# Decoder layer, last third: down projection product by product over all columns, first gate and up pair as plain products, all sums on VectorE

## Chip, core and metric

One core of a Trainium2 chip. The metric is the device time of one execution in microseconds (us), the median of several runs. Engines by the names of the profile: PE (TensorE matrix multiply), PEld (its weight loads), DVE (VectorE), ACT (ScalarE), POOL (GpSimd), SP (SyncE, whose queue issues all the DMAs).

## What is computed

One layer of a decoder trunk on x of 1024 tokens by 1024 channels in float32: a norm, one input projection, three attention mixers, a gated merge and an output projection with a residual, then a feed-forward block with a residual. The change lies in the last third, from the merge of the last mixer on:

```python
proj = jnp.einsum('btnm,nmd->btnd', branches, w_branch[l])
gates = jax.nn.sigmoid(cols['merge']).reshape(b, t, N_BRANCH, D_MODEL)
x = x + (gates * proj).sum(axis=2) @ w_out[l]
h = rms_norm(x, norm_ffn[l])
a = h @ w_gate[l]                                  # 1024 x 2816
a = causal_depthwise_conv(a, conv_w[l]) + conv_b[l]  # width 3 along the tokens
x = x + (gelu(a) * (h @ w_up[l])) @ w_down[l]      # 2816 x 1024
```

## The kernel before, in words

Everything is held transposed: 128 channels on the partitions, tokens along a row, so a tile is [128, 1024] and a column half is 512 tokens. Float32 products are made from two float32r parts of each operand: `hi` is a cast on ACT, `lo` the rest, a subtraction on DVE, and a product takes three matmuls (hi·hi, hi·lo, lo·hi) of 128x512.

From the feed-forward block on, a product of a 2x2 block matrix is made with seven block products instead of eight (the Strassen-Winograd scheme). The left blocks A11, A12, A21, A22 are of the weights, with the sums S1 to S4 of them; the right blocks B11 to B22 are of the activations, with the sums T1 to T4. `seven` (L1554) runs the seven products of one pair of output tiles: each product is `nk` steps of three matmuls, for gate and up nk = 4, so 7 x 4 x 3 = 84 matmuls. What comes out in PSUM is added up into u1, u2, u3 and the four output blocks on DVE and ACT. `left_ops` (L1520) loads the weights of one pair (two `qraw` tiles), makes S1 to S4 on POOL (L1543) and splits the seven left operands into `qhi` (ACT, L1547) and `qlo` (DVE, L1548), which lie in rings of seven. `right_ops` (L1498) makes T1 to T4 (L1512, on DVE and POOL) and splits them once for all pairs (L1419, L1420).

The stages of the last third, in order:
- `merge_last` (L1423): the last mixer's projection, gated on DVE (L1447), added to the merged sum on POOL (L1448), split.
- `out_proj` (L1452): the output projection with the residual, one half of the tokens after the other, h = 0 and h = 1. For each half squares are added up (`sqacc`), `rms_cols` sums them over the partitions with tiny matmuls (L326) and takes the power -1/2 on POOL (L329); `bcast_cols` spreads the result with four small DVE operations and matmuls and a copy on ACT (L337 to L339); then the norm multiplies x1 in place (L1482). The norm of the second half, and T1 to T4 that need both halves, stand between `out_proj` and the first pair.
- `gate_up` (L1614): 11 pairs f0 = 0, 2, ..., 20; in each a `seven` for gate, the convolution (ACT L1628, DVE L1631) and gelu, a `seven` for up, the multiplication (DVE L1650) and a store of the two tiles to DRAM (`s_act`, L1651). Of the first pair the products A11·B11 and A12·B21, which need the first half alone, are run early.
- `down` (L1671): the down projection in four groups of the 22 channel tiles (4, 6, 6, 6). In each group the activations are loaded back, `right_ops` makes and splits their sums, and for each of four m a `left_ops` and a `seven` with nk = 2 or 3 follow. The results are added to the residual in SBUF each time: six additions on DVE and three on POOL (L1572) in each of the 16 `seven`.

A scheduler sets the order of the instructions on each engine from dependences and its own estimate of durations; buffers (pools and rings) set the dependences. Each engine, the SP queue too, works off its own list in order.

Of the kernel before, what the change touches and what calls it, by code (L numbers as in the profile page):

```python
# [167 lines left out]
class Builder:  # L168
# [98 lines left out]
    def setup(self, ctx):  # L267
# [37 lines left out]
        self.right, self.sevens = {}, 0  # L305
# [1107 lines left out]

    def split(self, pool, tag, src):
# [4 lines left out]
        nc.scalar.copy(hi, src)  # L1419
        nc.vector.tensor_tensor(out=lo, in0=src, in1=hi.bitcast(F32), op=ALU.subtract)  # L1420
        return hi, lo

    def merge_last(self, n, macc, rp, wq, sp):  # L1423
# [13 lines left out]
        for cc in range(4):  # L1437
            w = self.quads(wq, a["w_branch"][n], cc * 256, 4)
            for h in range(2):
                hs = slice(h * 512, (h + 1) * 512)  # L1440
                for b in range(2):
                    j = cc * 2 + b
                    gt = self.t(sp, [P, 512], F32, "stage", 3)
# [4 lines left out]
                    nc.gpsimd.tensor_tensor(out=macc[j][:, hs], in0=macc[j][:, hs], in1=gt, op=ALU.add)  # L1448
# [3 lines left out]
    def out_proj(self, x1, sums, wq, sp):  # L1452

        nc, a = self.nc, self.a
        for h in range(2):
            hs = slice(h * 512, (h + 1) * 512)
            acc = self.t(sp, [P, 512], F32, "sqacc", 1)
            for cc in range(4):
                w = self.quads(wq, a["w_out"], cc * 256, KD)
                for b in range(2):  # L1460
                    j = cc * 2 + b
                    xr = self.t(sp, [P, 512], F32, "stage", 3)
# [8 lines left out]
                    else:  # L1471
                        sq = self.t(sp, [P, 512], F32, "sqh", 2)
# [4 lines left out]
            rbc = self.t(sp, [P, 512], F32, "rbc2", 1)  # L1477
            self.bcast_cols(sp, r, rbc)

            def normed(ks):  # L1480
                for k in ks:
                    nc.vector.scalar_tensor_tensor(out=x1[k][:, hs], in0=x1[k][:, hs], scalar=self.gffn[:, k:k + 1],  # L1482
                                                   in1=rbc, op0=ALU.mult, op1=ALU.mult)
                    if h == 0:
                        self.right["B11" if k < 4 else "B21", k % 4] = self.split(self.xp, f"xl{k}", x1[k][:, hs])

            normed(range(KD if h == 0 else 4))
        return lambda: normed(range(4, KD))

# [8 lines left out]
    def right_ops(self, rows, room, where, have=(), then=None):  # L1498


        nc = self.nc
        q = []
        for (top, bottom), t in zip(rows, room):
            q.append({"B11": top[:, 0:512], "B12": top[:, 512:1024], "B21": bottom[:, 0:512],
                      "B22": bottom[:, 512:1024], "t": t})
        sums = {"T1": ("B11", "B12", "B11", nc.vector if then else nc.gpsimd), "T2": ("t", "B22", "T1", nc.vector),
# [322 lines left out]
```

## Time and profile before

| | |
|---|---|
| time, median of 3 runs | 1954.72 us (1953.18 to 1955.0) |
| time of the profiled execution | 1955.4 us |
| its span | 1953.6 us |
| PE busy | 1866.3 us (96%), mean granted clock 0.98 |
| DVE / ACT / POOL busy | 1401.5 / 937.0 / 787.3 us |

The span is what the hardware profiler recorded on the core; the time of the same execution is 1.8 us longer. Views used below: the stage table (busy time of each engine in a stretch of the span, with the number of instructions in brackets, the granted TensorE clock, the DMA share and GB/s), the timeline (start, duration, engine, line, operation, and in brackets the idle time before it and what ended it), a line's own page (min/median/max duration in ns), and the table of waits. In all of them L is a line of the kernel.

### The profile page before, as it was taken

What the parts mean: (1) busy time and instruction counts of PE and PEld (TensorE: products, weight loads), DVE (VectorE), ACT (ScalarE), POOL (GpSimd) and SP (SyncE); (2) the same over time, 40 slices, a digit from 0 to 9 for tenths busy, and PEclk for the clock granted to TensorE, in tenths of its full rate; (3) what the DMA queues carried; (4) which work ended last, traced back from release to release, by engine and by line L of the source; (5) the groups of instructions that cost most, each with busy time, mean ns of one, the idle gap of its engine ahead of it and who ended that gap; (6) DMA issues with size and microseconds to landing.
All of it is one profiled execution on the core that took longest, in us unless ns stands there. A gap on an engine that the chain in (4) does not pass through costs nothing.

```text
span 1953.6 us, 30776 instructions
## 1 busy us (share of the span) xinstructions
PE 1866.3 (96%) x10651; PEld 1630.4 (83%) x10651; DVE 1401.5 (72%) x2747; ACT 937.0 (48%) x2030; POOL 787.3 (40%) x843
## 2 busy tenths in 40 slices
PE   8999999999999999999999999799999999879888
PEld 8999999999988888888788888578888888657667
DVE  7755677777767667576787675886665676899995
ACT  5434566564645546455775234343443344443341
POOL 2223645655503313032122530543332333488665
PEclk9999999999999999999999999899999999989889
DMA  6435223233231222213446555223222222522312
GB/s 209 132 112 137 71 81 80 83 86 93 63 89 47 62 79 67 75 49 88 134 122 188 176 173 163 91 65 130 71 92 87 76 77 85 204 83 80 113 33 103
DMA packets 188144, 197.71 MB, mean 101 GB/s; under 512 B 41441, under 2 KB 157169, under 8 KB 187988
## 3 DMA queue, kind: packets, MB, share of 16 engines
q1 hardware_dynamic: 187924, 195.61, 32.7%
q8 instruction: 84, 1.38, 0.3%
q14 instruction: 72, 0.59, 0.1%
q0 software_dynamic: 64, 0.13, 0.0%
HBM read 141.93 MB, written 53.76 MB: 100 GB/s over the span
## 4 chain that ended last, share of the span: by engine, by line
PE 81%; DVE 11%; issue 3%; DMA 2%; ACT 2%; POOL 1%; SPq 0%; POOLq 0%; DVEq 0%; ACTq 0%
PE D L259 9%; PE D L258 9%; PE D L260 9%; PE T L796 4%; PE S L1565 3%; PE S L1563 3%; PE S L1564 3%; PE T L1563 3%; PE T L1564 3%; PE T L1565 3%; PE O L820 2%; PE D L1565 2%; PE D L1563 2%; PE D L1564 2%; PE O L819 2%
## 5 line engine op out<-in xcount | busy, mean ns | idle before, releaser
L712 ACT ACTIVATE p<-S,mf 128x512 f32<-128x512 f32 (+3 forms) x320 | 174.1, 548 | 103.7 <-DVE mf L703 95.4
L761 POOL TENSOR_SCALAR p<-p,den,gates 128x384 f32<-128x384 f32 (+3 forms) x160 | 108.3, 688 | 271.0 <-DVE den L755 168.8
L804 DVE TENSOR_TENSOR pTl<-T,pTh 128x512 fp32r<-128x512 f32 (+2 forms) x248 | 150.8, 615 | 80.4 <-ACT pTh L803 78.5
L258 PE MATMUL D<-whi,xh 128*128 128x256 f32 (+2 forms) x680 | 199.6, 294 | 2.4 <-ACT whi L234 2.4
L259 PE MATMUL D<-wlo,xh 128*128 128x256 f32 (+2 forms) x680 | 193.2, 284 | 2.3 <-DVE wlo L235 2.3
L260 PE MATMUL D<-whi,xl 128*128 128x256 f32 (+2 forms) x680 | 192.7, 283 | 0.0
L803 ACT CAST pTh<-T 128x512 fp32r<-128x512 f32 (+2 forms) x248 | 128.1, 531 | 120.4 <-PE T L796 109.2
L259 PE MATMUL D<-xl,whi 128*128 128x512 f32 x448 | 176.6, 394 | 0.0
L1547 ACT CAST qhi<-qS 128x512 fp32r<-128x512 f32 (+2 forms) x152 | 85.5, 564 | 188.4 <-PE D L1564 62.0
L258 PE MATMUL D<-xh,whi 128*128 128x512 f32 x368 | 152.2, 414 | 0.0
L260 PE MATMUL D<-xh,wlo 128*128 128x512 f32 x368 | 145.0, 394 | 0.0
L761 POOL TENSOR_SCALAR p<-p,den 128x256 f32<-128x256 f32 (+3 forms) x160 | 88.7, 569 | 127.0 <-DVE den L755 44.5
L796 PE MATMUL T<-c,p 128*128 128x128 f32 x864 | 129.7, 273 | 6.3 <-POOL p L761 3.5
L1547 ACT CAST qhi<-qraw 128x512 fp32r<-128x512 f32 (+2 forms) x114 | 64.3, 564 | 147.8 <-PE S L1564 53.3
L1548 DVE TENSOR_TENSOR qlo<-qS,qhi 128x512 fp32r<-128x512 f32 (+2 forms) x152 | 124.6, 822 | 14.7 <-ACT qhi L1547 14.6
L258 PEld LDWEIGHTS D<-whi,xh 128*128 128x128 f32 x680 | 129.5, 190 | 4.6 <-ACT whi L234 3.0
L259 PEld LDWEIGHTS D<-wlo,xh 128*128 128x128 f32 x680 | 129.5, 190 | 3.8 <-DVE wlo L235 2.9
L260 PEld LDWEIGHTS D<-whi,xl 128*128 128x128 f32 x680 | 129.2, 190 | 0.0
L1548 DVE TENSOR_TENSOR qlo<-qraw,qhi 128x512 fp32r<-128x512 f32 (+2 forms) x114 | 102.1, 895 | 36.8 <-ACT qhi L1547 36.6
L235 DVE TENSOR_TENSOR wlo<-wraw,whi 128x512 fp32r<-128x512 f32 (+2 forms) x136 | 102.4, 763 | 31.8 <-ACT whi L234 28.6
L819 PE MATMUL O<-pTh,VV 128*128 128x256 f32 x448 | 119.2, 289 | 2.0 <-DVE osum L885 1.9
L820 PE MATMUL O<-pTl,VV 128*128 128x256 f32 x448 | 116.4, 284 | 2.2 <-DVE pTl L804 2.2
(405 smaller groups left out, 5775.1 us busy)
## 6 DMA issues: line engine op xcount, KB each, us to landing
wraw<-w_in SPq DMA_DIRECT2D x96, 256.0 KB
s_gate<-stage SPq DMA_DIRECT2D x48, 256.0 KB
stage<-s_gate SPq DMA_DIRECT2D x48, 256.0 KB
qraw<-w_gate SPq DMA_DIRECT2D x22, 512.0 KB
qraw<-w_up SPq DMA_DIRECT2D x22, 512.0 KB
s_act<-gc SPq DMA_DIRECT2D x22, 512.0 KB
qraw<-w_down SPq DMA_DIRECT2D x24, 384.0 KB
qraw<-w_out SPq DMA_DIRECT2D x16, 512.0 KB
```

Source lines behind the costliest of these rows:

```text
L258: nc.tensor.matmul(out, lh, rh, start=(k == 0), stop=False)
L259: nc.tensor.matmul(out, lh, rl, start=False, stop=False)
L260: nc.tensor.matmul(out, ll, rh, start=False, stop=(k == n - 1))
L712: nc.scalar.activation(pt, z["tiles"][n][:, :w], AF.Exp, bias=z["m"], scale=-1.0, accum_out=den[:, n, q:q + 1])
L761: nc.gpsimd.tensor_scalar(pt, pt, d0[:, q:q + 1], 1.0 if gate is None else gate, op0=ALU.mult, op1=ALU.mult)
L796: nc.tensor.transpose(p[:, c0:c0 + P], z["t"][:, k:k + P], self.ident)
L819: nc.tensor.matmul(ow, vv[:, kj, :], parts["h"][:, cs], start=(b_first and s == 0), stop=False)
L820: nc.tensor.matmul(ow, vv[:, kj, :], parts["l"][:, cs], start=False, stop=(b_last and s == len(bank) - 1))
L1548: nc.vector.tensor_tensor(out=lo, in0=src[n], in1=hi.bitcast(F32), op=ALU.subtract)
L1563: nc.tensor.matmul(p, lh[:, kk, :], rh, start=(first and kk == 0), stop=False, skip_group_check=True)
L1564: nc.tensor.matmul(p, lh[:, kk, :], rl, start=False, stop=False, skip_group_check=True)
L1565: nc.tensor.matmul(p, ll[:, kk, :], rh, start=False, stop=(kk == nk - 1), skip_group_check=True)
```

## The change

- `merge_last`: the addition to the merged sum goes from POOL to DVE; the loaded gates, and in `out_proj` the loaded residual, lie in the four `qS` tiles (`spare`) instead of a pool of three.
- `out_proj`: the factor of the norm is spread with one DVE operation (identity times the four columns) and one matmul, and stays in PSUM. While the norm of the second half is made, the plain block products (eight, not seven) of the pair f0 = 0 that need the first half alone are run, for up and for gate; then the norm; then the plain products of the second half. A plain pair takes 96 matmuls for gate and 96 for up. T1 to T4 are made after that, all on DVE.
- `left_ops`: S1 to S4 on DVE.
- `gate_up`: ten pairs from f0 = 2. In it, at f0 = 8 to 18 in program order, `down_sums` loads w_down a pair of row tiles at a time (`top`, `bottom` in the tiles xh4, xh5), makes the left sums S1 to S4 of all columns on DVE, and stores them to DRAM (`s_sums`).
- `down`: seven phases, each one block product over all 11 row tiles k and four m, with the four sums in PSUM (924 matmuls as before). A step k loads one left tile [128, 512] (from w_down or s_sums) into a `qS` tile and splits it and the right tile into the `qhi`/`qlo` rings of seven. The right operand is split again in each phase; its sums are made on DVE in place. Each of the results is taken from PSUM once per phase (`take`), 40 additions on DVE in all. The two last activation tiles stay in SBUF. The SP queue of this part is in the order of the program.

```diff
@@ merge_last
-                    gt = self.t(sp, [P, 512], F32, "stage", 3)
+                    gt = self.spare()
...
-                    nc.gpsimd.tensor_tensor(out=macc[j][:, hs], in0=macc[j][:, hs], in1=gt, op=ALU.add)
+                    nc.vector.tensor_tensor(out=macc[j][:, hs], in0=macc[j][:, hs], in1=gt, op=ALU.add)
@@ out_proj
-            rbc = self.t(sp, [P, 512], F32, "rbc2", 1)
-            self.bcast_cols(sp, r, rbc)
...
+            diag = both[:, hs].rearrange("p (q c) -> p q c", q=4)
+            nc.vector.tensor_tensor(out=diag, in0=self.ident.unsqueeze(1).to_broadcast([P, 4, P]),
+                                    in1=r.unsqueeze(2).to_broadcast([P, 4, P]), op=ALU.mult)
+            rbc = self.ps("O")
+            nc.tensor.matmul(rbc, self.ones, both[:, hs], start=True, stop=True)
+            if h == 1:
+                both_up = [self.t(wq, [P, 512], F32, f"u{n}", 1) for n in (2, 3)]
+                self.plain(self.left_ops(a["w_up"], 0, True), 0, both_up)
+                ga = self.gate_tiles(sp)
+                left = self.left_ops(a["w_gate"], 0, True)
+                self.plain(left, 0, [z[:, 2:514] for z in ga])
...
+        self.plain(left, 1, [z[:, 514:1026] for z in ga])
+        gc = self.convolve(0, ga, sp)
+        more_up = [self.t(wq, [P, 512], F32, "u1", 2) for _ in range(2)]
+        self.plain(self.left_ops(a["w_up"], 0, True), 1, more_up)
...
+        for n in (1, 2):
+            for k in range(4):
+                minus(x1[k][:, lo], x1[k if n == 1 else k + 4][:, hi], x1[k][:, lo])
+                self.right[f"T{n}", k] = self.split(rp, f"r{4 * n - 4 + k}", x1[k][:, lo])
...
@@ left_ops
-                    nc.gpsimd.tensor_tensor(out=src[n], in0=src[x], in1=src[y], op=op)
+                nc.vector.tensor_tensor(out=src[n], in0=src[x], in1=src[y], op=op)
@@ plain
+        for i in range(2):
+            p = self.dps()
+            self.prod(p, left[f"A{i + 1}1"], f"B1{j + 1}", True)
+            self.prod(p, left[f"A{i + 1}2"], f"B2{j + 1}", False)
+            self.nc.scalar.copy(dst[i], p)
@@ gate_up
+            if 8 <= f0 < 20:
+                for k in range((f0 - 8) * 11 // 12, (f0 - 6) * 11 // 12):
+                    self.down_sums(k)
+        return gc
+
+    def down_sums(self, k):
+        nc, w = self.nc, self.a["w_down"]
+        lo, hi = slice(0, 512), slice(512, 1024)
+        top, bottom = (self.t(self.xp, [P, T], F32, f"xh{n}") for n in (4, 5))
+        nc.sync.dma_start(top, w[k * P:(k + 1) * P, :])
+        nc.sync.dma_start(bottom, w[(k + NF // 2) * P:(k + NF // 2 + 1) * P, :])
+        for n, o, x, y, op in ((0, bottom[:, hi], top[:, hi], bottom[:, hi], ALU.add),
+                               (2, top[:, hi], top[:, lo], top[:, hi], ALU.subtract),
+                               (1, top[:, lo], bottom[:, hi], top[:, lo], ALU.subtract),
+                               (3, bottom[:, lo], bottom[:, lo], top[:, lo], ALU.subtract)):
+            nc.vector.tensor_tensor(out=o, in0=x, in1=y, op=op)
+            nc.sync.dma_start(self.s_sums[n, k], o)
@@ down
+        phases = [(1, "A11", "B11"), (2, "A12", "B21"), (5, "S1", "T1"), (6, "S2", "T2"), (4, "A22", "T4"),
+                  (7, "S3", "T3"), (3, "S4", "B22")]
+        def prepare():
...
+            z, k = steps.pop(0)
+            n, ln, rn = phases[z]
+            if rn == "B11" and k >= lead:
+                rows(k, lo)
+            if rn == "B21":
+                rows(nk + k, lo)
+            if spread and ((z * nk + k) % 4 < 3 or z == 2):
+                spread.popleft()()
+            l = left(ln, k)
...
+            r = halves(right[rn][k])
+            ready.append((halves(l), r))
...
+        for z, (n, ln, rn) in enumerate(phases):
+            if n != 2:
+                ps = [self.ps(g) for g in ("SSSO", "TTDD")[n in (5, 4, 3)]]
...
+            tail = 3 if z == 6 else 0
+            for k in range(nk - tail):
+                prepare()
+                ops = ready.popleft()
+                for m in range(4):
+                    mm(m, k, ops)
+            prepare()
+            for m in range(4):
+                for q in range(tail):
+                    mm(m, nk - tail + q, ready[q])
+                take(n, m, ps[m])
```

Three places of the order show what moves. Up to the middle of `merge_last` all the engines have the same rows in both kernels.

PE at the norm of the second half, before. Names: O is the PSUM tile of the norm, L326 the sum over the partitions, L338 the spreading, `xl` operands of the first half, `r` of the second.

```order
L1565 MATMUL S_15433<-xl_3322_15047,qlo_15430 128x512
L338 MATMUL O_15395<-c_6_69,bc_15396 128x128
L338 MATMUL O_15395<-c_6_69,bc_15399 128x128
L338 MATMUL O_15395<-c_6_69,bc_15402 128x128
L338 MATMUL O_15395<-c_6_69,bc_15405 128x128
L1563 MATMUL D_15597<-r_3417_15492,qhi_15576 128x512
```

The same place after the change; L1495 is the one matmul that spreads the factor.

```order
L1574 MATMUL D_15471<-xl_3308_15011,qlo_15456 128x512
L1495 MATMUL O_15371<-ga_14662,ones_73 128x512
L1572 MATMUL D_15471<-xl_3309_15015,qhi_15455 128x512
L1573 MATMUL D_15471<-xl_3309_15015,qhi_15455 128x512
L1574 MATMUL D_15471<-xl_3309_15015,qlo_15456 128x512
```

Before, the first matmul on the second half (`r`) is the next one after the spreading; after, 39 more matmuls on the first half (`xl`) follow the spreading before the first row with `r`.

DVE in the pairs of gate and up, before: splits of the weights (L1548), a sum of PSUM results (L1602, L1568), the multiplication (L1650).

```order
L1602 TENSOR_TENSOR u_3652_16582<-T_16598,u_3650_16580 128x512
L1568 TENSOR_TENSOR ga_16597<-u_3652_16582,D_16599 128x512
L1568 TENSOR_TENSOR ga_16597<-u_3652_16582,S_16652 128x512
L1548 TENSOR_TENSOR qlo_16852<-qS_3691_16839,qhi_16851 128x512
L1650 TENSOR_TENSOR gc_16530<-gc_16530,ga_16597 128x1024
```

DVE in the pair f0 = 4 after the change: L1660 is a sum of `down_sums`, L1563 one of S1 to S4, L1589 a sum of PSUM results, L1545 a split.

```order
L1660 TENSOR_TENSOR xh_3811_17574<-xh_3811_17574,xh_3810_17573 128x512
L1589 TENSOR_TENSOR u_3528_16103<-u_3526_16101,T_16105 128x512
L1545 TENSOR_TENSOR qlo_16374<-qS_3568_16361,qhi_16373 128x512
L1545 TENSOR_TENSOR qlo_16378<-qS_3569_16363,qhi_16377 128x512
L1545 TENSOR_TENSOR qlo_16382<-qraw_16359,qhi_16381 128x512
L1589 TENSOR_TENSOR ga_16058<-u_3528_16103,D_16106 128x512
L1589 TENSOR_TENSOR ga_16058<-u_3528_16103,O_16172 128x512
L1563 TENSOR_TENSOR qS_3599_16511<-qraw_16507,qraw_16509 128x512
L1660 TENSOR_TENSOR xh_3813_17586<-xh_3812_17585,xh_3813_17586 128x512
```

The sums of w_down, which the program has at f0 = 8 to 18, stand on DVE in the pairs f0 = 2 to 8, and between the last sum of one pair of row tiles and the first of the next there are seven other rows here. In all there are 11 such passages of four sums.

SP in the down projection, before: whole tiles of activations and of weights.

```order
L1693 DMA xl_4489_20366<-s_act_86 128x1024
L1693 DMA ga_20368<-s_act_86 128x1024
L1693 DMA r_4488_20365<-s_act_86 128x1024
L1531 DMA qraw_20124<-w_down 128x3x256
L1693 DMA xl_4490_20367<-s_act_86 128x1024
```

SP in the first phases of the down projection after the change.

```order
L1683 DMA r_4079_18866<-s_act_86 128x512
L1686 DMA xh_4087_18874<-s_x_20_85 128x512
L1695 DMA qS_4167_19180<-w_down 128x512
L1683 DMA xl_4080_18867<-s_act_86 128x512
L1686 DMA xh_4088_18875<-s_x_20_85 128x512
L1695 DMA qS_4172_19197<-w_down 128x512
```

A step of the first two phases has up to three loads of 256 KB; each waits on SP for its tile to be free.

More of the change, by code (lines that the diff above doesn't have):

```diff
@@ new lines, in out_proj @@
+            for j in range(KD):
+                k = j % 4
+                x = x1[j][:, hs]
+                nc.vector.scalar_tensor_tensor(out=x, in0=x, scalar=self.gffn[:, j:j + 1], in1=rbc,
+                                               op0=ALU.mult, op1=ALU.mult)
+                if h == 0:
+                    self.right["B11" if j < 4 else "B21", k] = self.split(self.xp, f"xl{j}", x)
+                else:
+                    self.right["B12" if j < 4 else "B22", k] = self.split(rp, f"r{8 + j}", x)
@@ L1495, with halves @@
+        for k in range(4):
+            minus(x1[k + 4][:, hi], x1[k + 4][:, hi], x1[k][:, hi])
+            minus(x1[k + 4][:, lo], x1[k + 4][:, lo], x1[k][:, lo])
+            self.right["T4", k] = self.split(self.xp, f"xh{k}", x1[k + 4][:, lo])
+        for k in range(4):
+            self.right["T3", k] = self.split(rp, f"r{8 + k}", x1[k + 4][:, hi])
     RIGHT = ("B11", "T1", "T2", "B21", "T3", "T4", "B22")
     LEFT = ("A11", "S1", "S2", "A12", "S3", "A22", "S4")
-    def right_ops(self, rows, room, where, have=(), then=None):
+    def halves(self, src, nk=4):
@@ L1501, in right_ops @@
         nc = self.nc
[L1502 to L1506, printed above, removed]
-                "T3": ("B12", "B22", "B12", nc.gpsimd), "T4": ("t", "B21", "T2", nc.gpsimd)}
-        for name in self.RIGHT:
-            if name in sums:
-                out, x, y, eng = sums[name]
-                for z in q:
-                    eng.tensor_tensor(out=z[out], in0=z[x], in1=z[y], op=ALU.subtract)
-                    z[name] = z[out]
-            if name not in have:
-                for kk, z in enumerate(q):
-                    self.right[name, kk] = self.split(*where(name, kk), z[name])
-            if name == "T1" and then:
-                then()
@@ new lines, in left_ops, with prod @@
+        for n in () if plain else self.LEFT:
+            if n in sums:
+                x, y, op = sums[n]
+                src[n] = self.t(self.wq, [P, 4, P], F32, "q" + n, 1)
+                nc.vector.tensor_tensor(out=src[n], in0=src[x], in1=src[y], op=op)
+        return {n: self.halves(src[n]) for n in (("A11", "A12", "A21", "A22") if plain else self.LEFT)}
+    def prod(self, p, left, rn, first):
+        nc = self.nc
+        lh, ll = left
+        for kk in range(4):
+            rh, rl = self.right[rn, kk]
+            nc.tensor.matmul(p, lh[:, kk, :], rh, start=(first and kk == 0), stop=False, skip_group_check=True)
+            nc.tensor.matmul(p, lh[:, kk, :], rl, start=False, stop=False, skip_group_check=True)
+            nc.tensor.matmul(p, ll[:, kk, :], rh, start=False, stop=(kk == 3), skip_group_check=True)
@@ L1616, in gate_up @@
+    def gate_up(self, sp):
         nc, a = self.nc, self.a
         hs = [slice(0, 512), slice(512, 1024)]
[L1619 to L1635 removed]
```

340 lines of the change are left out of this document (171 added, 169 removed).

## The prediction

> **What bounds the kernel now.** I read the page first, then a stage table from the norm on, then the timeline at the norm and the waits in the down projection. The page says that PE is nearly always busy, so time can come only from the places where it is not.
>
> ```profile
> span 1953.6 us, 30776 instructions
> PE 1866.3 (96%) x10651; PEld 1630.4 (83%) x10651; DVE 1401.5 (72%) x2747; ACT 937.0 (48%) x2030; POOL 787.3 (40%) x843
> ```
>
> The order of the instructions is the same up to the merge of the last mixer, so only what follows can change. The stage table has the norm of the second half with the first pair's start, the ten steady pairs, and the down projection.
>
> ```profile
> 1237.00:1290.00 53.00, 37.79 (x148) 29.30 (x147) 42.72 (x59) 20.79 (x36) 28.14 (x16) 0.81 0.13 40
> 1290.00:1660.00 370.00, 370.00 (x1634) 306.48 (x1634) 242.89 (x316) 149.43 (x219) 123.89 (x80) 1.00 0.27 87
> 1660.00:1953.60 293.60, 251.86 (x1014) 198.29 (x1012) 256.62 (x313) 106.96 (x209) 195.40 (x142) 0.93 0.30 103
> ```
>
> Columns: stretch, length, then PE, PEld, DVE, ACT, POOL busy (instructions), granted clock, DMA share, GB/s. In the middle row 1634 matmuls take 370 us without a wait: 0.2264 us each, the pitch that I use throughout. At this pitch the third row's 1014 would take 229.6 us, so 64.0 us are lost there. In the first row 21 of the 148 are not of the first pair (16 small ones of the norm and the last of the output projection); the other 127 would take 28.8 us, so 24.2 are lost. The middle stage loses nothing. Some 88 us in all can be won, no more.
>
> The timeline shows where the 24.2 us go.
>
> ```profile
> 1237.52 0.39 PE L260 MATMUL S<-r,qlo 128*128 128x512 f32 x1
> ...
> 1243.19 0.95 PE L326 MATMUL O<-ones,sqacc 128*128 128x1 f32 x8
> ...
> 1244.48 0.15 DVE L328 TENSOR_SCALAR rv<-O 128x4 f32<-128x4 f32 x1
> ...
> 1247.19 1.01 POOL L329 TENSOR_TENSOR r<-rv,mhalf 128x4 f32<-128x4 f32 x1
> ...
> 1250.94 5.39 DVE L1482 SCALAR_TENSOR_TENSOR xh<-xh,gffn,rbc 128x512 f32<-128x512 f32 x8 [1.23 <-ACT rbc L339]
> 1256.25 2.49 DVE L1512 TENSOR_TENSOR xh<-xh 128x512 f32<-128x512 f32 x4
> ...
> 1257.64 1.22 PE L1563 MATMUL D<-r,qhi 128*128 128x512 f32 x2 [7.35 <-ACT r L1419]
> ```
>
> The output projection ends at 1237.5. The factor is ready at 1250.9, DVE then multiplies eight tiles and makes T1, and PE has only 24 matmuls (5.4 us) to bridge this. The four sums in a row end after 2.49 us though one lasts 0.68: the pitch of a 128x512 operation on DVE is (2.49 - 0.68)/3 = 0.60 us.
>
> In the down projection the waits of PE (total us, times, longest) are short ones, most of them on DVE, and DVE's operations (min/median/max ns) are of two lengths.
>
> ```profile
> PE T L1564 <- DVE r L1420: 8.2, 3, 3.1
> PE S L1563 <- ACT u L1585: 6.1, 2, 3.3
> PE D L1565 <- DVE qlo L1548: 4.7, 2, 3.4
> ...
> L1420 DVE TENSOR_TENSOR r<-xl,r x13: 677/1177/1784, 1666.8 to 1894.2; 128x512 fp32r<-128x512 f32 x13
> L1420 DVE TENSOR_TENSOR r<-r,r x6: 677/1480/1494, 1741.8 to 1892.0; 128x512 fp32r<-128x512 f32 x6
> ...
> L1572 POOL TENSOR_TENSOR xh<-xh,u 128x512 f32<-128x512 f32 x48 | 73.0, 1537 | 42.4 <-DVE u L1597 22.3 <-DVE u L1602 18.4 <-PE S L1564 1.6
> ```
>
> The same split takes 0.68 us or 1.5 to 1.8; the third stage row has POOL busy for 195 of 294 us and DVE for 257. DVE, slowed while POOL adds, is the engine that PE waits for at the start of each of the four groups, where all right operands must be made at once.
>
> **The change, part by part.** The sum is made against the profiled execution, 1955.4 us (span 1953.6 and 1.8 around it).
>
> *Merge and output projection.* Sixteen additions go to DVE: 16 x 0.60 = 10 us over some 44 us in which DVE has room, and no matmul waits for them sooner than before. Nothing, between -1 and +1.
>
> *More matmuls.* Plain products need 96 instead of 84, for gate and up: 24 x 0.2264 = +5.4 us.
>
> *The norm.* PE has 96 matmuls on the first half, 21.7 us, behind the output projection. In the order 57 of them and the column sums stand ahead of the spreading matmul: the factor is there at 12.9 + 1 = 14 us after the projection's end (before: 13.4). DVE multiplies all eight tiles (5.4), then makes four more operations up to the first split of the second half (2.4): 21.8. PE reaches that operand at 14 + 39 x 0.2264 = 22.8. So the wait closes, barely. Next come 96 interleaved matmuls, 2.7 us for each step against 1.2 on DVE. Behind them T1 to T4 are due; their 16 sums and 16 splits are 19 us of DVE under 21.7 us of PE, but T4 comes last, behind part of the convolution. I take 3 us of waits left (1 to 8): 24.2 - 3 = -21.2 us.
>
> *Ten pairs.* PE stays at 38.0 us a pair (168 x 0.2264). DVE has 242.89 x 38.0/370 = 24.9 us of work a pair; S1 to S4 add 8 x 0.60 = 4.8, and in the pairs f0 = 2 to 8 up to twelve sums of w_down add 7.2: 36.9, or some 33 if the gain from a quiet POOL and the pitch are counted. DVE nearly full, in order, and its sums wait for a loop over memory: the last sum is stored, the two tiles are loaded again, the next four sums follow. The rows nearest to a store and a load are these: the last store of the output, and a load of weights with the POOL operation that waited for it.
>
> ```profile
> 1949.74 0.69 DVE L1568 TENSOR_TENSOR xh<-xh,S 128x512 f32<-128x512 f32 x1 [1.62 <-POOL xh L1572]
> ...
> 1948.57 2.22 SPq L1707 DMA_DIRECT2D outT<-xh  x2
> ...
> 1458.41 0.37 SPq L1531 DMA_DIRECT2D qraw<-w_gate  x1
> ...
> 1462.23 1.29 POOL L1543 TENSOR_TENSOR qS<-qraw,qraw 128x512 f32<-128x512 f32 x1 [4.43 <-DMA qraw<-w_gate]
> ```
>
> The store starts when DVE ends, 1950.4, and the span ends at 1953.6: about 3.1 us for 256 KB. The load took 1458.4 to 1462.2, 3.8 us for 512 KB. Store and load are 6.9 us; the order quoted has seven operations between two passages, 4.2 us. DVE, and all that is queued behind that sum (splits, PSUM sums for which PE waits), is short by 2.7 us in such a place. If all 11 passages were, and nothing absorbed it: 30 us. Other gaps are longer in the order, and DVE's room is 1 to 5 us a pair, so I take half of the passages and 11 us of room: +5 us (0 to 30; not below zero, since PE loses nothing there now).
>
> *Down projection.* PE does 924 matmuls as before, 209.2 us. DVE: 77 steps with two splits, 44 right sums, 40 additions: 238 x 0.60 = 143 us, with no POOL beside it; ACT has 154 casts. The sums of a phase are spread over its steps (2.7 us of PE each), and two rings of seven hold three steps and a half, 9.5 us. Narrowest are the starts of the fourth, fifth and seventh phases, ahead of which 8, 8 and 12 additions fall due (up to 8.2 us at 0.68): within those 9.5 us. Loads: in the first two phases about 56 of 256 KB, 14.7 MB in 60 us, 245 GB/s.
>
> ```profile
> 10.00:15.00 5.00, 5.00 (x45) 5.00 (x44) 5.00 (x5) 4.66 (x8) 0.98 (x2) 1.00 1.07 381
> ...
> 1694.00:1698.00 4.00, 3.86 (x18) 2.85 (x16) 1.02 (x2) 1.49 (x4) 0.73 (x1) 1.00 0.88 263
> 1698.00:1702.00 4.00, 0.98 (x3) 0.58 (x4) 2.76 (x5) 0.13 (x1) 0.20 (x1) 1.00 1.03 409
> 1702.00:1706.00 4.00, 4.00 (x12) 3.08 (x12) 4.00 (x7) 0.84 (x3) 2.65 (x3) 0.57 1.03 402
> ```
>
> This kernel moves up to 409 GB/s, so 245 fit. The page on DMA in the Trainium skill (DMA: Bandwidth & Descriptors, Bandwidth) speaks against this part: it wants transfers of 1 MiB or more for three quarters of the peak, and its table gives 138 GB/s at 64 KB and 341 at 1 MB; by the lower one the two phases would take 106 us, not 60, and the sum would be 46 us higher. The last two rows also show that behind a stretch in which PE stood for 3 us the clock fell to 0.57; where it stood for 0.14 us (1694:1698) it kept 1.00. The Trainium skill (TensorE: Matmul & The Clock Gate, Part 1) puts the limit at an idle window of about 3.4 us; by it the waits that I leave cost no clock, and longer ones would cost the same again.
>
> Of the 64.0 us lost here 6.3 lie behind the last matmul (1947.3 to 1953.6), and 57.7 are waits. I leave 5 of these (2 to 20): -52.7. The end becomes one addition and one store, 0.7 + 0.1 + 3.1 and a hop, 4.3: -2.0.
>
> Sum: 1955.4 + 5.4 - 21.2 + 5 - 52.7 - 2.0 = 1889.9, and 0.7 less against the median of 1954.72, which the profiled execution exceeds by as much: 1889.2, so **1889 us**.
>
> **The rivals.**
> - *The memory loop of the sums holds DVE in the pairs.* All 11 passages short, 30 us instead of 5: 1914 us. For it: a DVE that is 87 to 97% full and in order. Against it: the longer gaps elsewhere, and the loads of the next tiles can start when the first store is done.
> - *The norm stays open.* The cover was 1 us in my reckoning; if the splits of the second half come late and the clock falls, 24 us stay: 1910 us, the extra matmuls being paid for little. Against it: 21.7 us of cover instead of 5.4.
> - *The down projection stays bound by DVE at the changes of phase.* If each of the six holds PE for the additions due there (0, 4, 8, 8, 4, 12), 36 x 0.68 = 24 us instead of 5: 1908 us. For it: the waits on DVE of today. Against it: the rings, which hold 9.5 us.
> - *Slower: transfers of 256 KB in the down projection pass one after another.* 133 loads (77 left tiles, 40 halves of activations, 16 of the residual) at 3.1 us are 412 us instead of 214 (209 and the waits left): 198 us more, 2087 us. It decides from 280 us on (214 and the 66 us won), that is from 2.1 us a load, 125 GB/s. Against it: the rows above, and 381 GB/s in a stretch of the kernel's start.
>
> **How the numbers follow.** Forecast 58%, with 1878 to 1903 from the ends of the norm, the loop and the down projection; memory loop 18%; norm 7%; changes of phase 12%; transfers 5%. The range 1878 to 1925 holds the first four with some of them added up, and leaves the fifth and double mishaps out. Within 0.2% (3.9 us, about what a measurement can tell; the three runs before lie 1.8 us apart) is 1%, a part of the fifth case; slower 4%; faster 95%.
>
> **What would show it.** Right: no wait of PE over 3 us after the projection's end, DVE operations of 128x512 near 0.68 us throughout, 924 matmuls of the down projection in 209 to 220 us, POOL idle there. Wrong: PE waits for the sums S or for `qlo` in the pairs f0 = 2 to 8 with DVE waiting for a DMA into xh4 or xh5; DMA share near 1 in the first two phases; a low clock behind the norm.

## The result and the profile after

The changed kernel takes 1894.07 us (median of 4 runs, 1888.64 to 1899.45), beside it the kernel before 1954.86 (1953.18 to 1955.12): a ratio of 0.9691, interval 0.9662 to 0.9719. The forecast was 1889 within 1878 to 1925. The profiled execution took 1894.6 us, its span 1892.8. (In the runs below one execution of e9 ran at a granted clock of 0.75 from end to end and took 2285.6 us; it is left out, and since it was the recorded one, e9 has no profile to compare.)

The head of the page and the same three stages as before, columns as in the prediction:

```profile
span 1892.8 us, 30670 instructions
PE 1847.5 (98%) x10663; PEld 1623.0 (86%) x10663; DVE 1345.5 (71%) x2825; ACT 926.1 (49%) x1987; POOL 406.2 (21%) x586
```

```profile
1237.00:1290.00 53.00, 53.00 (x238) 43.61 (x237) 42.25 (x69) 28.78 (x50) 1.01 (x1) 1.00 0.22 65
1290.00:1660.00 370.00, 362.05 (x1585) 297.75 (x1584) 286.29 (x430) 142.11 (x210) 0.00 (x0) 1.00 0.45 148
1660.00:1892.80 232.80, 227.05 (x1000) 187.02 (x998) 161.17 (x253) 96.76 (x163) 0.00 (x0) 1.00 0.49 158
```

The first stage now has no gap. The second has one that was not there before: 1585 matmuls in 370 us where there were 1634, 49 x 0.2264 = 11.1 us. In the third 1000 matmuls are worth 226.4 of 232.8 us, so 6.4 us are lost there instead of 64.0. POOL does nothing in the last two.

The waits of PE between 1310 and 1670, and from 1670 to the end (total us, times, longest), are few:

```profile
PE T L1572 <- DVE u L1589: 8.0, 5, 3.2
...
PE S L1789 <- DVE qlo L1545: 1.0, 1, 1.0
PE S L1787 <- ACT qhi L1544: 0.5, 1, 0.5
```

The norm of the second half, in the timeline: the last matmul of the output projection, the column sums, the spreading, the multiplication, the first split of the second half on DVE, and the first matmul that uses it.

```profile
1239.39 0.39 PE L260 MATMUL S<-r,qlo 128*128 128x512 f32 x1
...
1246.19 0.95 PE L327 MATMUL O<-ones,gc 128*128 128x1 f32 x8
...
1253.49 1.02 PE L1495 MATMUL O<-ga,ones 128*128 128x512 f32 x2
...
1255.22 4.70 DVE L1506 SCALAR_TENSOR_TENSOR xh<-xh,gffn,O 128x512 f32<-128x512 f32 x7
...
1261.63 0.69 DVE L1426 TENSOR_TENSOR r<-xh,r 128x512 fp32r<-128x512 f32 x1
...
1263.23 0.39 PE L1572 MATMUL S<-r,qhi 128*128 128x512 f32 x1
```

DVE has the split at 1262.3, PE comes to it at 1263.2: the cover closes with 0.9 us to spare, and the last row shows no idle time.

The first 30 us of the down projection in the stage table, then DVE's splits of the left tiles (min/median/max ns), then the last matmul and the last addition in the timeline:

```profile
1683.00:1713.00 30.00, 30.00 (x134) 24.85 (x133) 23.04 (x36) 15.52 (x27) 0.00 (x0) 1.00 0.80 274
```

```profile
L1545 DVE TENSOR_TENSOR qlo<-qS,qhi x157: 682/691/721, 1281.5 to 1880.8; 128x512 fp32r<-128x512 f32 x157
```

```profile
1888.13 0.39 PE L1789 MATMUL D<-qhi,qlo 128*128 128x512 f32 x1
...
1888.56 0.69 DVE L1679 TENSOR_TENSOR xh<-xh,D 128x512 f32<-128x512 f32 x1 [0.38 <-PE D L1789]
```

134 matmuls in 30 us is full pitch while 274 GB/s come in, the activations and left tiles in pieces of 256 KB. The splits, before of two lengths, now take 682 to 721 ns, all of them. From the end of the last matmul (1888.5) to 1892.8 are 4.3 us.

**Where the new gap lies.** Between 1300 and 1500, in five stops of 1.43, 1.04, 1.56, 0.76 and 3.16 us (the 8.0 above) and in the matmuls behind them. These are the rows around the largest stop, from SP, DVE and PE:

```profile
1438.48 0.33 SPq L1655 DMA_DIRECT2D xh<-w_down  x1
...
1443.56 0.69 DVE L1660 TENSOR_TENSOR xh<-xh,xh 128x512 f32<-128x512 f32 x1 [2.25 <-DMA xh<-w_down]
...
1444.28 0.33 SPq L1661 DMA_DIRECT2D s_sums<-xh  x1
...
1450.82 1.74 SPq L1683 DMA_DIRECT2D xh<-s_act  x4
1452.66 0.38 SPq L1556 DMA_DIRECT2D qraw<-w_gate  x1
...
1458.72 0.69 DVE L1563 TENSOR_TENSOR qS<-qraw,qraw 128x512 f32<-128x512 f32 x1 [3.54 <-DMA qraw<-w_gate]
1459.34 0.68 DVE L1589 TENSOR_TENSOR u<-u,T 128x512 f32<-128x512 f32 x1
...
1460.17 0.47 PE L1572 MATMUL T<-r,qhi 128*128 128x512 f32 x1 [3.16 <-DVE u L1589]
```

DVE waits twice. First for a tile of w_down that was issued at 1438.5 and is there at 1443.6. Then for weights that SP issued only at 1452.7: SP's list had a store that waited for DVE (1444.28), then four loads of activations whose tiles had to be stored out first (1450.82). Behind DVE's wait stands the sum of PSUM results (L1589) for which PE waits. The four other stops end with the same L1589, each within 5 us of the first sum of a passage; DVE had waited 0.76, 3.29, 0.59 and 3.02 us ahead of these four sums. DVE's longest waits for transfers between 1300 and 1500 (total us, times, longest):

```profile
DVE xh L1660 <- DMA xh<-w_down: 7.7, 5, 2.2
DVE xh L1660 <- DMA s_act<-gc: 6.3, 2, 3.3
DVE qS L1563 <- DMA qraw<-w_gate: 3.5, 1, 3.5
```

The first two rows are one thing, the waits ahead of the first sum of a passage, 14.0 us in 7 of the 11 passages. (The table names what came last by the profile. In e1 below, whose DVE list is the same, it puts one of the two waits of the second row down to the load of w_down.) So there are two suspects: the staging's own loop (load, sums, store, load), and SP, which stands at the stores while others' loads queue behind.

### The profile page after: what moved, and what is told of

It is laid out like the page before. It is cut to its first block, busy times and chain, and to the rows that moved or that the text cites. A ratio compares the mean times of both kernels' runs of the same rounds, so it can differ in the third digit from the quotient of the medians.

```text
span 1892.8 us, 30670 instructions
## 1 busy us (share of the span) xinstructions
PE 1847.5 (98%) x10663; PEld 1623.0 (86%) x10663; DVE 1345.5 (71%) x2825; ACT 926.1 (49%) x1987; POOL 406.2 (21%) x586
## 4 chain that ended last, share of the span: by engine, by line
PE 78%; DVE 10%; DMA 6%; issue 3%; ACT 2%; POOL 1%; SPq 0%; DVEq 0%; ACTq 0%; POOLq 0%
PE D L259 9%; PE D L258 9%; PE D L260 9%; PE T L797 4%; PE O L821 2%; PE S L685 2%; PE O L820 2%; PE S L259 2%; PE S L260 2%; PE S L258 2%; PE S L689 2%; PE S L1789 2%; PE S L1787 2%; PE S L1788 2%; PE S L1573 1%
## 5 line engine op out<-in xcount | busy, mean ns | idle before, releaser
L1544 ACT CAST qhi<-qS 128x512 fp32r<-128x512 f32 x157 | 97.4, 622 | 207.4 <-PE O L1788 57.1
L260 PE MATMUL D<-whi,xl 128*128 128x256 f32 (+2 forms) x680 | 192.7, 283 | 0.0
L1545 DVE TENSOR_TENSOR qlo<-qS,qhi 128x512 fp32r<-128x512 f32 x157 | 107.8, 691 | 54.1 <-ACT qhi L1544 53.6
L260 PE MATMUL D<-xh,wlo 128*128 128x512 f32 x368 | 145.0, 394 | 0.0
L260 PEld LDWEIGHTS D<-whi,xl 128*128 128x128 f32 x680 | 129.3, 190 | 0.0
L685 PE MATMUL S<-U,X 128*128 128x256 f32 (+2 forms) x320 | 107.8, 342 | 4.8 <-ACT p L713 4.7
L797 PEld LDWEIGHTS T<-c,p 128*128 128x128 f32 x864 | 101.1, 141 | 12.5 <-POOL p L762 7.8
```

Source lines behind the costliest of these rows:

```text
L260: nc.tensor.matmul(out, ll, rh, start=False, stop=(k == n - 1))
L685: nc.tensor.matmul(p, z["x"][:, z["qs"]], u[:, ks], start=True, stop=False)
L797: nc.tensor.transpose(p[:, c0:c0 + P], z["t"][:, k:k + P], self.ident)
```

## The experiments

Besides each median the table gives a length: from the start of the last matmul of the output projection (L260 of the changed kernel) to the span's end in the profiled execution. What comes ahead of it is nearly the same in all, but this matmul starts anywhere from 1235.1 to 1240.5 us, so differences of 2 us are better read in the length. "Staged sums" are the left sums of `down_sums`. Two cautions hold for all rows. The kernels of e2 and e3 leave out part of the layer's computation. And an edit also gives the scheduler another order: behind the output projection, DVE's list in e1 is that of the changed kernel, and in e3, e4 and e6 it is another one.

| run | edit | median us | length us |
|---|---|---|---|
| before | | 1954.9 to 1956.2 | 716.1 |
| changed | | 1894.1 | 653.4 |
| e1 | the changed kernel again | 1893.3 | 652.7 |
| e2 | no staged sums | 1881.3 | 642.0 |
| e3 | staged sums not stored | 1885.5 | 646.8 |
| e4 | staging on POOL's queue | 1886.9 | 646.5 |
| e5 | staging over nine pairs | 1899.2 | 659.3 |
| e6 | staging in two pairs of tiles | 1884.1 | 644.5 |
| e7 | first pair with seven products | 1901.8 | 662.7 |
| e8 | before, sums on VectorE | 1925.7 | 684.6 |
| e9 | staging over seven pairs | 1888.0 | |
| e10 | e4 and e6 together | 1892.8 | 652.3 |
| e11 | changed, sums on POOL | 1909.7 | 667.3 |
| e12 | changed, S1 to S4 on POOL | 1904.6 | 667.2 |

### e1: the changed kernel again

> The changed kernel itself, once more, as the measure for the other runs beside it. Its four executions so far lay between 1888.6 and 1899.5 us, eleven apart, where the kernel before stayed within two. Theory (the memory loop of the left sums sets DVE back in the pairs f0 = 2 to 8 by an amount that varies with the landing times of transfers): the spread stays, 1888 to 1900, and every loss of over 1 us in the pairs lies between 1340 and 1480. Rival (something later in the span varies): pairs without a loss in one execution and a lossy down projection in it.

1893.25 us, 1890.06 to 1894.88 in five runs, ratio 0.9677 (0.9663 to 0.9691). The kernel before spread over 5.5 us in the nine runs beside it, so the spread is no mark of the change. In the recorded execution 1588 matmuls stand between 1290 and 1660, 46 short of full; 45 of them between 1360 and 1480: the loss is reproduced in its place.

### e2: without the staged sums

```diff
-            if 8 <= f0 < 20:
-                for k in range((f0 - 8) * 11 // 12, (f0 - 6) * 11 // 12):
-                    self.down_sums(k)
...
-                src = self.s_sums[int(name[1]) - 1, k]
+                src = a["w_down"][k * P:(k + 1) * P, lo]
```

> Leaves out the left sums of the down projection (S1 to S4 of w_down are not made; the phases that use them read the left quarter of w_down instead), so DVE has 44 operations less, SP 66 transfers less, and all else is the same. Theory (the loss between 1340 and 1480 is made by the staging): the pairs run at full pitch, 1894 - 12 = 1882 us, 1880 to 1884, and the spread between executions falls to about 2 us. Rival (S1 to S4 of gate and up on DVE are what fills it, the staging costs nothing beside them): 1890 to 1894, with the missing matmuls still there.

1881.27 us, ratio 0.9619 (0.9605 to 0.9632). The stretch that lost 11 us, in this kernel:

```profile
1300.00:1500.00 200.00, 200.00 (x884) 165.62 (x883) 142.06 (x210) 77.89 (x116) 0.00 (x0) 1.00 0.28 90
```

884 matmuls are full pitch. The staging makes the whole loss, and S1 to S4 of gate and up on DVE cost nothing by themselves. The spread did not fall to 2 us (1878.96 to 1882.74).

### e3: sums without stores

```diff
             nc.vector.tensor_tensor(out=o, in0=x, in1=y, op=op)
-            nc.sync.dma_start(self.s_sums[n, k], o)
...
-                src = self.s_sums[int(name[1]) - 1, k]
+                src = a["w_down"][k * P:(k + 1) * P, lo]
```

> The 44 left sums of w_down are made as in the changed kernel, and their tiles loaded, but they are not stored (the phases read the left quarter of w_down instead): DVE has all its work, the loop over memory is cut to the loads. Theory A (the loop store - load - next sums holds DVE): most of the loss goes, 1882 to 1886 us. Theory B (DVE is simply full with 44 more operations, 44 x 0.60 = 26 us in four pairs): 1891 to 1896 us, as with the stores, with DVE busy and without its waits for the DMA into xh4 and xh5.

1885.46 us (ratio 0.9647, 0.9630 to 0.9665), theory A. DVE does all its sums and is busier than in the changed kernel (161.73 us there in the same stretch), yet PE has 863 matmuls instead of 835:

```profile
1300.00:1500.00 200.00, 196.34 (x863) 161.32 (x863) 166.80 (x252) 77.17 (x114) 0.00 (x0) 1.00 0.42 140
```

By the length 6.6 of 11.4 us go with the stores. The remaining 21 matmuls (4.8 us) lie with what stays, DVE's 44 sums and their loads; this run doesn't part these two. Since the stores are also what SP stands at, it doesn't part the two suspects either.

### e4: the staging's transfers on POOL's queue

```diff
-        nc.sync.dma_start(top, w[k * P:(k + 1) * P, :])
-        nc.sync.dma_start(bottom, w[(k + NF // 2) * P:(k + NF // 2 + 1) * P, :])
+        nc.gpsimd.dma_start(top, w[k * P:(k + 1) * P, :])
+        nc.gpsimd.dma_start(bottom, w[(k + NF // 2) * P:(k + NF // 2 + 1) * P, :])
...
-            nc.sync.dma_start(self.s_sums[n, k], o)
+            nc.gpsimd.dma_start(self.s_sums[n, k], o)
```

> The loads and stores of the left sums go to the queue of POOL, which has nothing else to do there, instead of SP's; DVE's work and the loop over memory stay. Theory A (the loop's own length holds DVE): no change, 1890 to 1896 us, and DVE still waits for the DMA into the two tiles. Theory C (SP stands at a store that waits for DVE, 39 us in 37 waits in the trace, and the loads of gate and up weights queued behind it come late): 1884 to 1889 us, and the waits for qraw and s_act go.

1886.88 us (0.9648, 0.9634 to 0.9662), as theory C has it. The waits of SP between 1300 and 1500, of the changed kernel:

```profile
SPq L1661 <- DVE xh L1660: 39.3, 37, 3.3
SPq L1661 <- DMA xh<-w_down: 36.3, 10, 4.9
SPq L1556 <- DVE qlo L1545: 30.4, 15, 12.7
```

and of this one:

```profile
SPq L1556 <- DVE qlo L1545: 127.4, 21, 18.6
SPq L1643 <- DVE gc L1641: 46.0, 8, 11.0
```

SP now stands at the loads of weights, for their tiles to be free, that is, it is early with them. DVE waits as long as before for the staging's loads (14.6 us in 6 waits, against the 14.0 in 7), so the loop has not become shorter, and PE still gains 30 matmuls (865). One part of what C named did not come: DVE's waits for qraw did not go (7.1 us, against 4.5). So the run fits a cost of SP's queue, but it doesn't show that late weights are how the queue costs time, and DVE's other order is a rival that no run here rules out.

### e6: two pairs of tiles

```diff
-            ua = [self.t(self.xp, [P, T], F32, f"xh{6 + i}") for i in range(2)]
+            ua = [self.t(self.xp, [P, T], F32, t) for t in self.pair(f0)]
...
-            if 8 <= f0 < 20:
-                for k in range((f0 - 8) * 11 // 12, (f0 - 6) * 11 // 12):
+            if f0 <= 12:
+                for k in range(f0 - 2, min(f0, 11)):
                     self.down_sums(k)
...
+    turn = 0
...
+    def pair(self, f0):
+        self.turn += 1
+        n = 4 if self.turn % 2 == 0 and f0 <= 12 else 6
+        return [f"xh{n}", f"xh{n + 1}"]
...
-        top, bottom = (self.t(self.xp, [P, T], F32, f"xh{n}") for n in (4, 5))
+        top, bottom = (self.t(self.xp, [P, T], F32, t) for t in self.pair(0))
```

> The staging keeps SP's queue but alternates between two pairs of tiles (xh4, xh5 and xh6, xh7, which it shares with the up products), two passages to a pair from f0 = 2 to 12, so that the loads of one passage need not wait for the stores of the one just before. Theory A (length of the loop store - load): 1883 to 1887 us. Theory C (SP stands at stores that wait for DVE, and what is queued behind them is late, whatever the tiles): 1889 to 1896 us, with SP's waits at the stores as long as before.

1884.13 us (0.9631, 0.9617 to 0.9646): in the range of theory A, and the fastest of the runs that compute the whole layer, 9 to 10 us below the changed kernel. SP's waits at the stores, and the one wait that PE has between 1300 and 1500:

```profile
SPq L1668 <- DVE xh L1667: 36.8, 35, 5.8
...
SPq L1668 <- DMA xh<-w_down: 19.3, 4, 5.2
```

```profile
PE D L1572 <- DVE ga L1589: 0.7, 1, 0.7
```

This does not show that the loop's length is the cause. SP's waits at a load for the store before it did fall, from 17.6 us to 5.7, but so did its waits at the stores, from 75.6 us to 56.1. The 11 passages are spread wider too: their first and last sums start at 1297 and 1516 us, in the changed kernel at 1298 and 1447. And DVE waited longer for the staging's loads, 20.0 us against 14.0. So e4 and e6 each take away more than half of the same loss; which of these differences does it in e6 stays open.

### e10: both together

> The fourth and the sixth run together: two pairs of tiles in turn, two passages to a pair from f0 = 2 to 12, and POOL's queue. Alone the queue won some 6 us and the tiles some 9 against the changed kernel, of 12 that the staging costs. Theory (both cure the same wait, the tiles' way from store to load): 1881 to 1885 us, no better than the better of the two by more than 2. Rival (two different causes, which add up): 1878 to 1880 us.

The edit is that of e4 on top of that of e6. 1892.76 us (0.9675, 0.9661 to 0.9690): no better than the changed kernel. Both expectations fall. A load of w_down on POOL's queue and the sum that waits for it, in this kernel:

```profile
1419.78 0.55 POOL L1661 DMA_DIRECT2D xh<-w_down  x1 [3.87 <-DVE gc L1641]
...
1428.05 0.69 DVE L1667 TENSOR_TENSOR xh<-xh,xh 128x512 f32<-128x512 f32 x1 [6.32 <-DMA xh<-w_down]
```

The tile, shared with the up products, is free only after their multiplication (L1641); the load then takes 8.3 us to be there, and DVE stands for 6.3 of them, in a list whose order is fixed. In all DVE waits 37.7 us for such loads between 1290 and 1700, against 20.0 in e6. The load took 8.3 us here and about 5 in the rows above. Between 1421 and 1426 the DMA share is 0.86 to 1.10 at 279 to 392 GB/s, so it shared the DMA engines with other transfers; that this is the whole reason was not tested.

### e5 and e9: the staging spread over more pairs

The tiles of a pair are those its up products have just left, so that no passage can be pulled ahead; POOL's queue as in e4. e5 takes nine pairs (e9 has seven, `f0 < 16` and 14 in place of 18):

```diff
-            if 8 <= f0 < 20:
-                for k in range((f0 - 8) * 11 // 12, (f0 - 6) * 11 // 12):
-                    self.down_sums(k)
+            if f0 < 20:
+                for k in range((f0 - 2) * 11 // 18, f0 * 11 // 18):
+                    self.down_sums(k, f0)
...
+    def pair(self, f0):
+        n = 6 if f0 % 4 == 0 else 4
+        return [f"xh{n}", f"xh{n + 1}"]
```

> The sums of w_down on POOL's queue as in the fourth run, and spread over nine pairs (f0 = 2 to 18) instead of the first four: the two tiles of a pair are those which its up products have just left (xh4, xh5 and xh6, xh7 in turn), so no passage can be pulled ahead. DVE's work is the same. Theory (what is left in the fourth run, some 18 missing matmuls or 4 us, is a DVE that is full in four pairs and waits for reloaded tiles there): those go, 1881 to 1883 us, as without the sums. Rival (each passage costs something wherever it stands): 1886 to 1888 us, the losses spread over nine pairs.

1899.18 us (0.9710, 0.9696 to 0.9724), slower than the changed kernel, and not for the reason of either side. In the pairs PE is at 90 matmuls in each 20 us up to 1640, as the theory had it, although DVE waits 24.1 us there for the staging's loads, in nine waits of up to 3.75 us: more than in the changed kernel. With one or two passages to a pair, they cost PE nothing. The time goes at the entry to the down projection; PE's longest stops, the last staged sum and its store, and SP's first load of activations:

```profile
1670.55 0.68 DVE L1664 TENSOR_TENSOR xh<-xh,xh 128x512 f32<-128x512 f32 x1
...
1671.53 0.54 POOL L1665 DMA_DIRECT2D s_sums<-xh  x1 [1.86 <-DVE xh L1664]
...
1671.67 4.71 SPq L1687 DMA_DIRECT2D xh<-s_act  x4
...
1671.97 0.76 PE L1572 MATMUL D<-r,qhi 128*128 128x512 f32 x1 [7.78 <-DVE xh L1589]
1682.42 0.79 PE L1791 MATMUL S<-qhi,qhi 128*128 128x512 f32 x1 [5.77 <-ACT qhi L1544]
```

The last passage is still at work when the last up products need DVE: their sums (L1589) stand behind it in DVE's list. And it lies in xh4 and xh5, where the first activations of the down projection go: SP, whose list is in the order of the program there, stands at the first of these loads until the last store, with the loads of all left tiles behind it.

> The fifth run's staging (tiles of the up products in turn, POOL's queue), but over f0 = 2 to 14 instead of 2 to 18, so that xh4 and xh5 are free before the down projection loads into them. Theory (the fifth run lost its time at the start of the down projection alone, where the loads of activations waited for the last passages, and nothing in the pairs): 1880 to 1883 us, with 90 matmuls in each 20 us of the pairs and the first loads of activations on time. Rival (seven pairs with one or two passages are again too full): 1884 to 1890 us, with missing matmuls in the pairs.

1883.9 to 1889.3 us, ratio 0.9646 (0.9631 to 0.9661): with the staging done by f0 = 14, 11 of e5's us come back, which fits the account of where they went. It did not reach the 1880 to 1883 us of the theory and lies in the rival's range, and without a comparable profile it stays open where the rest is.

### e7: the first pair with seven products

The edit takes out all the lines of `plain` from `out_proj` (the run of both halves, the convolution and the store) and lets `gate_up` begin at f0 = 0.

> The plain first pair undone: f0 = 0 is a pair of seven products like the others, and the norm of the second half has no matmuls but those that the scheduler pulls ahead of it; down projection and sums as changed. Theory (the cover of 21.7 us by plain products is the whole gain at the norm, less 5.4 us for 24 more matmuls): PE stands for 18 to 24 us behind the output projection, 1893 + 19 = 1912 us, 1907 to 1916. Rival (the one spreading matmul in place of the small DVE operations, and DVE without POOL beside it, shorten the norm itself, so that most of the gain stays): 1896 to 1905 us.

1901.80 us (0.9725, 0.9710 to 0.9740). PE's two long stops and the granted clock (the column behind POOL) in and after them:

```profile
1258.75 1.22 PE L1557 MATMUL D<-r,qhi 128*128 128x512 f32 x2 [5.80 <-ACT r L1425]
...
1266.53 0.80 PE L1558 MATMUL D<-r,qhi 128*128 128x512 f32 x1 [6.55 <-DVE r L1426]
```

```profile
1255.00:1262.00 7.00, 1.22 (x2) 0.50 (x2) 7.00 (x13) 4.68 (x9) 0.00 (x0) 0.59 0.00 0
1262.00:1270.00 8.00, 3.47 (x9) 2.76 (x9) 8.00 (x14) 0.79 (x2) 0.00 (x0) 0.51 0.00 0
```

From the projection's end (1240.7) to 1290 PE runs 129 matmuls of the pairs, 29.2 us of 49.3: 20.1 us are lost, as the theory has it. Counted in the same way, from its own projection's end, the kernel before loses 23.5 (127 matmuls from 1237.7 on) and the changed kernel 1.7 (215 from 1239.6 on). So the plain pair wins 18.4 us and pays 5.4, and the 3.4 between 23.5 and 20.1 are what the rival said of a shorter norm. By its time the run lies in the rival's range: it is only 8.5 to 9.3 us slower than the changed kernel, where the theory had 19, since the norm is shorter and since its pairs miss 34 matmuls and not 49 (3.4 us less): the staging meets another order.

### e8, e11, e12: the sums between POOL and VectorE

e8 is the kernel before with `nc.gpsimd` turned to `nc.vector` in the sums of `right_ops`, of `left_ops` and of the residual; e11 the changed kernel with `left_ops` and the right sums of the down projection turned to `nc.gpsimd`; e12 with `left_ops` alone:

```diff
-                nc.vector.tensor_tensor(out=src[n], in0=src[x], in1=src[y], op=op)
+                nc.gpsimd.tensor_tensor(out=src[n], in0=src[x], in1=src[y], op=op)
```

> The kernel before with nothing changed but the engine: every sum that POOL makes in the feed-forward block (S1 to S4, T1, T3, T4, the additions to the residual) goes to DVE. Theory P (DVE slowed by POOL beside it is the loss in the down projection, so a quiet POOL wins most of the 58 us there): 1905 to 1930 us. Theory O (the order by block products wins it, as it has fewer operations and spreads them: in the old order DVE would have about 313 + 142 = 455 operations of 0.60 us, 273 of 294 us, and stay full at the four group starts): 1945 to 1975 us. In both DVE's operations of 128x512 fall to 0.68 us.

1925.71 us (0.9846, 0.9828 to 0.9863): theory P. Two groups of DVE operations in the down projection, of the kernel before (splits of weights, and additions of a PSUM result; the third column is busy us, mean ns):

```profile
L1548 DVE TENSOR_TENSOR qlo<-qS,qhi 128x384 fp32r<-128x384 f32 (+2 forms) x65 | 59.6, 920 | 0.1
...
L1568 DVE TENSOR_TENSOR xh<-xh,D 128x512 f32<-128x512 f32 x32 | 21.6, 676 | 0.7 <-PE D L1565 0.7
```

the same in e8, and its stage:

```profile
L1548 DVE TENSOR_TENSOR qlo<-qS,qhi 128x384 fp32r<-128x384 f32 (+1 forms) x64 | 32.7, 514 | 0.4 <-ACT qhi L1547 0.2
...
L1568 DVE TENSOR_TENSOR xh<-xh,D 128x512 f32<-128x512 f32 x32 | 21.6, 676 | 2.7 <-PE D L1565 2.7
```

```profile
1660.00:1922.80 262.80, 235.35 (x983) 186.58 (x981) 241.12 (x440) 102.56 (x199) 0.00 (x0) 0.96 0.34 113
```

The operations that read two tiles in SBUF fall from 920 to 514 ns; those that read PSUM were 676 and stay so. (Both means of the splits mix two widths, in the same shares. Those of 384 columns alone, 48 in each kernel, fall from 945 to 546 ns.) DVE has 127 operations more (440 against 313) and is busy for 241 us instead of 257. The stage loses 262.8 - 983 x 0.2264 = 40.2 us instead of 64.0. Most of the rest of the gain lies at the norm: from the projection's end to 1290, 15.6 us are lost instead of 23.5. Theory O failed in its idea that a full DVE can't win: at 92% it is still less late.

> The changed kernel with S1 to S4 of gate and up and the right sums of the down projection on POOL, the order of the work as changed. Theory P (POOL's additions slow DVE's beside them from 0.68 to 1.2 to 1.8 us, and DVE, which carries the staging, has no room for that): 1900 to 1930 us, DVE's operations of two lengths again. Rival (the 124 sums taken off DVE are worth more than the slowing costs): 1880 to 1890 us.

1909.71 us (0.9761, 0.9747 to 0.9775), theory P. In the down projection (1660 to 1906.0) 1041 matmuls are worth 235.7 of 246.0 us, so 10.3 are lost there, against 6.4 in the changed kernel.

> The changed kernel with S1 to S4 of gate and up alone on POOL; down projection all on DVE. Theory P: the pairs with the staging lose more than now, 1896 to 1912 us, and the down projection is as in the changed kernel. Rival (relief of DVE in the pairs): 1882 to 1890 us, fewer than 30 matmuls missing between 1300 and 1500.

1904.63 us (0.9736, 0.9722 to 0.9750), theory P; the stage of the pairs of e12, in which 112 matmuls are missing (25.4 us; 94 in e11):

```profile
1290.00:1660.00 370.00, 352.81 (x1522) 286.93 (x1522) 268.62 (x339) 135.63 (x202) 115.80 (x74) 0.99 0.43 141
```

The four kernels make a square: with the old order 1956 on POOL and 1925.7 on VectorE, with the new one 1909.7 and 1893.3. (In e11 the additions of results to the residual and those of the merge stay on VectorE.) The engine alone is worth 30 us in the old order and 16 in the new; the order and the plain pair together 46 with POOL's sums and 32 without.

## Why the prediction came out as it did

*More matmuls, +5.4.* The count bears it out: 24 at 0.2264.

*The norm, -21.2 with 3 us of waits left.* No wait was left. The whole working can be laid beside the rows: the factor at 14 us behind the projection (14.9 measured, 1239.6 to 1254.5), the first split at 21.8 (22.7), PE there at 22.8 (23.6). The stages do not begin alike, as the projection ends at 1237.7 before and at 1239.6 after; counted from there to 1290 the loss is 23.5 and 1.7 us (e7 above), so 21.8 are won. (The prediction's 24.2 took the projection's last matmuls as lost.) The rival of an open norm is out; e7 shows what it would have been.

*The memory loop, +5 (0 to 30).* This is the term that was mis-sized. It is 11.1 us in the profiled execution, and e2 shows that the staging makes all of it. The working put half of the 11 passages at 2.7 us, 15 us in all, and let 11 us of DVE's room take up most of it. The waits came out about as reckoned: 14.0 us in 7 passages, 0.6 to 3.3 us each. What failed is the room: DVE works off its list in order, the PSUM sums for which PE waits stand behind the late passage, and PE stopped five times. The working also left out SP, which stood 36 and 39 us at the stores while weights queued behind them (the largest stop follows such weights, and e4 wins 7 us by length with DVE's waits for the staging's loads unchanged), and it left out that a stop costs more than its length: 8.0 us of stops, 11.1 lost. One sign of being right failed, as PE has a wait of over 3 us (3.16), and one of being wrong came in part: DVE waits for a DMA into xh4 and xh5 in these pairs, though PE then waits for a PSUM sum and not for S or `qlo`. How the 11.1 us divide between the loop and SP's queue stays open, since e3 and e6 change both and e4 also changes DVE's order. The rival that all passages are short gave 30 and was too high.

*Down projection, -52.7 with 5 us left.* 6.4 us are lost in the stage, 4.3 of them behind the last matmul: 2.1 are left, -55.6. The changes of phase cost PE nothing. The cause given, a DVE slowed by POOL, is shown by e8, but it is not the whole of the 57.6 us won there. With the engine changed first (e8), it wins 23.8 and the order by block products the other 33.8. With the order changed first (e11, where the additions to the residual are on DVE too), the order wins 53.7 and the engine 3.9. So the two cures overlap, and the prediction didn't part them.

*The end, -2.0.* 6.3 to 4.3 us, as forecast.

*Transfers one after another.* Out: 274 GB/s at full matmul pitch. The Trainium skill (DMA: Bandwidth & Descriptors, Bandwidth), by which 46 us more were reckoned, wants 1 MiB for three quarters of the peak; this trace does not bear out that cost for transfers of 256 KB.

Put together: 1953.6 + 5.4 - 21.8 + 11.1 - 55.6 - 2.0 = 1890.7. The measured span is 1892.8. Of the 2.1 between, 1.9 are the part ahead, which ended at 1239.6 instead of 1237.7. So two terms came out 3.5 us better than forecast, one 6.1 worse, and the rest is the part of the kernel ahead of the norm. That the total came within 5 us owes something to luck: these errors have opposite signs.

## What to carry to other kernels

An elementwise operation that is moved to an idle engine is not free if it slows the busy one: before spreading sums over two engines, compare the durations of the same operation beside the helper and without it. A store that waits for a busy engine holds everything behind it in its queue, so new staging wants a look at what is queued behind its stores, and tiles that the next stage doesn't need first. When a cure is found, run it alone and together with the others: here two good ones gave nothing together.

## What the runs showed of the hardware

- POOL's additions stretch only those DVE operations that read two tiles in SBUF, not those with a PSUM operand. In the down projection of the kernel before, the splits of 384 columns with a POOL addition beside them all along took 1172 ns on average (35 of them, 546 to 1643), those with none beside them 546 (22 of them); the additions of a PSUM result took 677 and 680 ns. The Trainium skill (GPSIMD Engine Reference, Key points) names this condition, two SBUF inputs, and the rows agree.
- Behind the stop of 3.16 us the granted clock (last column but two) fell to 0.50 for a time:

```profile
1460.00:1462.00 2.00, 1.83 (x5) 1.37 (x6) 2.00 (x5) 0.59 (x1) 0.00 (x0) 0.70 0.03 8
1462.00:1464.00 2.00, 2.00 (x6) 1.57 (x5) 2.00 (x3) 0.00 (x0) 0.00 (x0) 0.50 0.00 0
1464.00:1466.00 2.00, 2.00 (x9) 1.60 (x9) 1.97 (x4) 0.62 (x1) 0.00 (x0) 0.94 0.51 209
```

  20 matmuls run here in 6 us instead of 26, some 1.5 us more. The four stops of 0.76 to 1.56 us left the clock at 1.00. The prediction cited a limit of about 3.4 us; these traces show no single limit. In e11 the clock is 0.50 from 1341 to 1344, behind a stop of 2.27 us that ended at 1339.6, and in e12 it stays at 1.00 behind one of 2.43 us that ended at 1352.4. (The ends of the matmuls are modelled, so the stops may be a little longer than recorded.)
